# Expert weights in 12 places instead of 19 after the second block, with the side work as a background task

## The chip, the cores and the metric

The kernel runs on one core of a Trainium2 chip. The metric is the device time of one execution in microseconds (us), the median of three runs. Engines: PE is TensorE (matrix products), PEld its weight loads, DVE is VectorE, ACT is ScalarE, POOL is GpSimd, and SP is SyncE, whose queue issues the weight loads. Each engine executes its own instructions in the order in which the program lists them. Everything is float32.

## What is computed

A first block of two layers (a mixer, a cross attention to a memory of 256 rows, and a mixture of 32 experts) and a second block of four layers (pooling, neighbourhood attention, convolution, pooling), on 256 rows of width 1024. What the change touches is below: the cross attention's keys and values of `mem`, the experts, and the pooling layer of the second block's context `ctx`, which depends on no result of the first block.

```python
def memory_cross_attention(x, mem, wq, wk, wv, wo):
    q = to_heads(x @ wq, XATTN_HEADS)
    k = to_heads(mem @ wk, XATTN_HEADS)
    v = to_heads(mem @ wv, XATTN_HEADS)
    logits = jnp.einsum('bhqd,bhmd->bhqm', q, k).astype(jnp.float32) * (XATTN_HEAD_DIM ** -0.5)
    p = jax.nn.softmax(logits, axis=-1).astype(v.dtype)
    return from_heads(jnp.einsum('bhqm,bhmd->bhqd', p, v)) @ wo
...
def hierarchical_moe(x, w_group, b_group, w_expert, b_expert, w_gate, w_up, w_down):
    def one_sequence(xs):
        s = xs.shape[0]
        g_logits = (xs @ w_group + b_group).astype(jnp.float32)
        g_idx = jnp.argmax(g_logits, axis=-1)
        g_weight = jnp.take_along_axis(jax.nn.softmax(g_logits, axis=-1), g_idx[:, None], axis=-1)
        e_logits = (xs @ w_expert + b_expert).astype(jnp.float32).reshape(s, N_GROUPS, EXPERTS_PER_GROUP)
        e_logits = e_logits[jnp.arange(s), g_idx]
        top_val, top_idx = lax.top_k(e_logits, TOP_K_IN_GROUP)
        top_w = jax.nn.softmax(top_val, axis=-1) * g_weight
        expert_id = g_idx[:, None] * EXPERTS_PER_GROUP + top_idx
        gates = jnp.einsum('ske,sk->se', jax.nn.one_hot(expert_id, N_EXPERTS, dtype=jnp.float32), top_w).astype(xs.dtype)
        hid = jax.nn.silu(jnp.einsum('sd,edf->sef', xs, w_gate)) * jnp.einsum('sd,edf->sef', xs, w_up)
        return jnp.einsum('sef,efd->sd', hid * gates[:, :, None], w_down)

    return lax.map(one_sequence, x)
...
def first_block(x, mem, ...):
    ...
    for l in range(DEPTH):
        ...
        x = layer_norm(DEEPNORM_ALPHA * x + mix, ln_mix_g[l], ln_mix_b[l])
        xa = memory_cross_attention(x, mem, xattn_wq[l], xattn_wk[l], xattn_wv[l], xattn_wo[l])
        x = layer_norm(DEEPNORM_ALPHA * x + xa, ln_mem_g[l], ln_mem_b[l])
        ff = hierarchical_moe(x, router_group_w[l], router_group_b[l], router_expert_w[l], router_expert_b[l],
                              expert_w_gate[l], expert_w_up[l], expert_w_down[l])
        x = layer_norm(DEEPNORM_ALPHA * x + ff, ln_ffn_g[l], ln_ffn_b[l])
    return x
...
def _pool_mixer(h, w_in, w_grp, scale, w_out):
    u, g = jnp.split(h @ w_in, 2, axis=-1)
    b_, l_, _ = u.shape
    ug = u.reshape(b_, l_, N_POOL_GROUPS, POOL_GROUP)
    pooled = jnp.stack([_centred_mean(ug[:, :, i], w) for i, w in enumerate(POOL_WINDOWS)], axis=2)
    mixed = jnp.einsum('blgc,gcd->blgd', pooled - ug, w_grp).reshape(b_, l_, WIDTH)
    return (mixed * scale * jax.nn.silu(g)) @ w_out
...
def second_block(x, c, ctx, c_ctx, ...):
    last_ctx_reader = max([i for i in range(DEPTH_2) if i % N_MIXERS_2 == 1], default=-1)
    for i in range(DEPTH_2):
        kind, j = i % N_MIXERS_2, i // N_MIXERS_2
        update_ctx = i < last_ctx_reader
        shift, scale, gate = _modulation(c, ada_w[i], ada_b[i])
        hx = _rmsnorm(x, norm_g[i]) * (1.0 + scale[:, None]) + shift[:, None]
        if kind == 1 or update_ctx:
            cshift, cscale, cgate = _modulation(c_ctx, ada_w[i], ada_b[i])
            hc = _rmsnorm(ctx, norm_g[i]) * (1.0 + cscale) + cshift
        if kind == 0:
            yx = _pool_mixer(hx, pool_w_in[j], pool_w_grp[j], pool_scale[j], pool_w_out[j])
            if update_ctx:
                yc = _pool_mixer(hc, pool_w_in[j], pool_w_grp[j], pool_scale[j], pool_w_out[j])
        elif kind == 1:
        ...
        x = x + gate[:, None] * yx
        if update_ctx:
            ctx = ctx + cgate * yc
    return _rmsnorm(x, final_g)
```

## The kernel before

**Products.** A float32 weight is split into a high and a low part (`whi` by ACT, `wlo` by DVE, L307 and L308), the activations likewise (`xth`, `xtl`), and TensorE makes three products of them. The experts' weights (`w`) are used without a split, in one product. Sums land in PSUM banks; while the experts run, four banks hold the result (`acc`), two serve the main work (`ps`) and two the side work (`pl`).

**Weights.** All weights come in granules of 1 MiB (128x2048), in a fixed order, the plan, which is the order in which the program asks for them. `pump` (line 265) issues a load on the SP queue for each next granule as long as `place` (line 259) finds a place for it. A ring has 8 places, a second ring (`ring2`) 7, and there are 4 boxes. `in_ring2` and `in_box` (lines 249 and 252) give the latter two to expert granules alone, and only if the granule's part of its stage, by `part` (line 255), fits the present one. An expert's gate, up and down are three granules. `used` (line 275) frees a place once the instruction that reads it last has been written, and calls `pump`, so that a load is issued behind those instructions, and waits for them on the chip.

**An expert stage.** `moe(l)` (line 1487) runs once per layer, l = 0 and 1, here the first and the second stage. It has eight blocks (`q`), each with the four experts of one group. For each block TensorE does the gate and up products (128 matmuls, `xg`), the gather of the rows of the next block (`disp`, `xp`), some small transposes, and the down products (`w`, `y`) that add into `acc`. A block takes up to 32 rows an expert at once. If an expert has more, an extra round runs under an `If` (L1537 for gate and up, L1586 for down), whose branches are executed on every engine.

While the first four blocks run, the 8 + 4 + 7 = 19 places are open. At `q == 3` (line 1547) the right side of SBUF is closed and reopened with a pool of split weights (6 pairs) and one of 16 half rows (`more`); in the second stage the boxes are closed and reopened too. From there on there are 12 places. The test in `part` puts the same border into the plan: the gate and up granules of expert 16 and later and the down granules of expert 12 and later belong to a stage's second half.

**Side work.** In the first stage this is `mem_early`: the memory's transposes and its K and V products for the second layer. In the second stage it is `ctx_in` and `pool_ctx`: the whole pooling layer of the context, up to the transposed context (`ctn`) that the neighbourhood layer starts from. `between(n)` (line 1505) runs one piece of it at written places: pieces 9, 11, 13, 15, 17 and 19 in the first stage, 3, 6, 7 and 10 to 21 in the second, where n = 3q stands behind the gate and up of block q, 3q + 1 behind its gather and 3q + 2 behind its down. All of it is written ahead of the last block's down.

**Order elsewhere.** `Flow` (line 86) writes the program as tasks that yield a modelled cost and a lag, and takes the ready task of the lowest priority number. A task that is not ready gives way to another. The modulation products (`ada`, L366 with `w,cT`) are such tasks with priority 2. Two of them concern the change: the last third of `ada(0)` is held until the first router (`ev_router[0]`), and `ada(1)` is spawned at `q == 7` of the first stage.

## Time and profile before

| | |
|---|---|
| median of 3 runs | 1782.72 us (1778.27 to 1784.91) |
| profiled execution | 1784.17 us, its span 1782.4 us |
| PE busy | 1585.1 us, 89% of the span |
| PEld busy | 1230.3 us, 69% |
| DVE busy | 925.4 us, 52% |
| ACT busy | 701.8 us, 39% |
| POOL busy | 166.2 us, 9% |
| DMA | 427.14 MB, mean 240 GB/s |

The span is the time that the profiler saw from the first instruction to the last; the execution's own time has 1.8 us around it. Shares of busy time are means over stages with different limits. The first expert stage lies between 312.69 and 578.17 us, the second between 861.22 and 1198.71 us. In a timeline row the second number is the time from the start of a group of like instructions to its end, and the bracket tells how long the engine was idle ahead of it and what ended that. [...]

### The profile page before, as it was taken

To read this page: it belongs to the slowest core of one execution; us is meant where nothing else is said; L and a number is where in the kernel's file an instruction comes from. 1 tells how busy PE (TensorE), PEld (TensorE's weight loads), DVE (VectorE), ACT (ScalarE), POOL (GpSimd) and SP (SyncE) were. 2 spreads that over 40 slices of the span, in tenths; PEclk is the share of its full clock that TensorE was granted. 3 is DMA by queue.
4 is the path that set the end of the run, shared out by engine and by line. 5 is a ranking of instruction groups with operands and counts; after the bars stand their busy time and mean duration, and the time that the engine had idled before them with its cause. 6 is when DMAs were issued, how large, how long until landed. Compare 5 with 4: busy or idle time off the path is not lost. (4 is left out here: it accounts for less than half of the span.)

```text
span 1782.4 us, 29217 instructions
## 1 busy us (share of the span) xinstructions
PE 1585.1 (89%) x11357; PEld 1230.3 (69%) x11357; DVE 925.4 (52%) x2162; ACT 701.8 (39%) x1422; POOL 166.2 (9%) x248
## 2 busy tenths in 40 slices
PE   7999997778898699989688898978999998999997
PEld 6766986555664566677555576748978886699786
DVE  5567646262132846665321324358455566566645
ACT  4654541112221354433011232344545565445543
POOL 5000301000000400030100000001002122000101
PEclk9989998999999899899799999999999999999999
DMA  8356657899978945476459598796458765575630
GB/s 307 96 189 214 204 221 288 361 395 384 409 284 336 371 150 172 142 269 243 201 205 410 228 410 340 309 407 226 143 165 180 157 114 70 174 275 168 242 100 24
DMA packets 145951, 427.14 MB, mean 240 GB/s; under 512 B 12252, under 2 KB 19652, under 8 KB 121172
## 3 DMA queue, kind: packets, MB, share of 16 engines
q1 hardware_dynamic: 140660, 411.19, 62.1%
q0 software_dynamic: 5088, 13.32, 5.6%
q8 instruction: 118, 1.93, 0.4%
q14 instruction: 85, 0.70, 0.1%
HBM read 423.43 MB, written 1.05 MB: 238 GB/s over the span
## 5 line engine op out<-in xcount | busy, mean ns | idle before, releaser
L308 DVE TENSOR_TENSOR wlo<-w,whi 128x512 fp32r<-128x512 f32 (+2 forms) x586 | 394.7, 709 | 260.0 <-ACT whi L307 257.6
L307 ACT CAST whi<-w 128x512 fp32r<-128x512 f32 (+2 forms) x592 | 341.4, 610 | 241.7 <-PE ps L366 193.1
L366 PE MATMUL ps<-xth,whi 128*128 128x256 f32 x896 | 262.4, 293 | 7.2 <-DVE x L1610 3.8
L366 PE MATMUL ps<-xth,wlo 128*128 128x256 f32 x896 | 257.7, 288 | 4.9 <-DVE wlo L308 4.9
L366 PE MATMUL ps<-xtl,whi 128*128 128x256 f32 x896 | 257.5, 287 | 0.8 <-DVE xtl L1146 0.8
L366 PE MATMUL ps<-whi,xth 128*128 128x512 f32 (+2 forms) x512 | 207.1, 405 | 4.4 <-ACT whi L307 4.0
L366 PE MATMUL ps<-wlo,xth 128*128 128x512 f32 (+2 forms) x512 | 199.2, 389 | 0.4 <-DVE wlo L308 0.4
L366 PE MATMUL ps<-whi,xtl 128*128 128x512 f32 (+2 forms) x512 | 198.9, 388 | 0.2 <-DVE xtl L1146 0.2
L366 PEld LDWEIGHTS ps<-xth,whi 128*128 128x128 f32 x896 | 174.4, 195 | 16.6 <-ACT whi L307 10.6
L366 PEld LDWEIGHTS ps<-xth,wlo 128*128 128x128 f32 x896 | 173.4, 194 | 5.8 <-DVE wlo L308 5.8
L366 PEld LDWEIGHTS ps<-xtl,whi 128*128 128x128 f32 x896 | 173.6, 194 | 3.4 <-issue 1.4
L366 PEld LDWEIGHTS ps<-whi,xth 128*128 128x128 f32 x512 | 99.4, 194 | 32.4 <-ACT whi L307 6.5
L366 PEld LDWEIGHTS ps<-whi,xtl 128*128 128x128 f32 x512 | 98.8, 193 | 20.7 <-DVE xtl L1146 0.9
L366 PEld LDWEIGHTS ps<-wlo,xth 128*128 128x128 f32 x512 | 99.4, 194 | 18.3 <-DVE wlo L308 1.4
L366 PE MATMUL ps<-w,xg 128*32 128x256 f32 x1536 | 90.8, 385 | 10.4 <-issue 3.7
L366 PE MATMUL ps<-w,y 128*32 128x512 f32 (+1 forms) x784 | 80.0, 546 | 8.5 <-DVE y L1455 4.9
L366 PEld LDWEIGHTS ps<-w,xg 128*32 128x32 f32 x1536 | 52.7, 111 | 47.9 <-issue 9.6
L1439 DVE TENSOR_TENSOR y<-y,ps 128x256 f32<-128x256 f32 x12 | 5.1, 422 | 120.8 <-ACTq L1537 76.9
L1146 POOL TENSOR_TENSOR xtl<-aff,xth 128x512 fp32r<-128x512 f32 x9 | 11.6, 1287 | 600.6 <-ACT xth L1145 600.6
L366 PE MATMUL ps<-disp,xp 128*128 128x128 f32 x384 | 52.5, 301 | 16.2 <-DVEq L1537 6.8
L366 PEld LDWEIGHTS ps<-disp,xp 128*128 128x128 f32 x384 | 50.7, 215 | 20.0 <-issue 13.3
L366 PEld LDWEIGHTS ps<-w,y 128*32 128x32 f32 x784 | 25.2, 113 | 50.6 <-issue 36.0
(517 smaller groups left out, 2510.7 us busy)
## 6 DMA issues: line engine op xcount, KB each, us to landing
w<-in_expert_w_gate_dram SPq DMA_DIRECT2D x64, 1024.0 KB, 14.2
w<-in_expert_w_up_dram SPq DMA_DIRECT2D x64, 1024.0 KB, 16.0
w<-in_expert_w_down_dram SPq DMA_DIRECT2D x64, 1024.0 KB, 11.4
w<-in_ada_w_dram SPq DMA_DIRECT2D x48, 1024.0 KB, 5.7
w<-in_pool_w_in_dram SPq DMA_DIRECT2D x24, 1024.0 KB, 11.0
w<-in_na_w_in_dram SPq DMA_DIRECT2D x24, 1024.0 KB, 6.3
w<-in_w_in_dram SPq DMA_DIRECT2D x16, 1024.0 KB, 11.4
w<-in_conv_w_in_dram SPq DMA_DIRECT2D x16, 1024.0 KB, 5.8
```

Source lines behind the costliest of these rows:

```text
L307: self.nc.scalar.copy(hi, src)
L308: (self.nc.gpsimd if self.spare and k % 2 else self.nc.vector).tensor_tensor(lo, src, hi.bitcast(F32), OP.subtract)
L366: self.nc.tensor.matmul(out, lhsT, rhs, start=start, stop=stop, skip_group_check=True)
L1146: (nc.gpsimd if j == 2 else nc.vector).tensor_tensor(lo, fs[j - 1], hi.bitcast(F32), OP.subtract)
L1439: nc.vector.tensor_tensor(h, sg, p[:, 256:512], OP.mult)
```

## The change

`SWITCH = 1`: the pools change behind the second block's gate and up (`q == 1`), no longer behind the fourth's, and `part` moves its border to gate and up of expert 8 and down of expert 4. From there 12 places serve the other six and a half blocks. `landing`, `landed` and `arrival` model when a granule arrives: 2.35 us after the one before it, or 2.2 + 2.35 us after its place came free, whichever is later. Ahead of each block's gate and up the main task yields until eight granules have arrived by that model, and ahead of the down until four have. The side work is no longer written in pieces at given places: `mem_early` and `pool_ctx` (which takes in `ctx_in`) are tasks of priority 2, spawned at the switch, that run where the main task yields. At the end of a stage the main task waits until the side task is written. Splits ahead of their use (`_ahead`) are allowed by the modelled landing. The last third of `ada(0)` has no hold, and `ada(1)` is spawned at the start of the second layer. Outside the expert stages one set of eight PSUM banks takes the place of two sets of four.

```diff
@@ -31,12 +31,13 @@
+SWITCH = 1
+DMA_STEP = 2.35
+DMA_LAG = 2.2
...
-EARLY_V = True
-MEM_AT = (9, 11, 13, 15, 17, 19)
@@ -254,7 +256,7 @@
-        return 2 * key[2] + (key[3] >= (12 if key[1] == "expert_w_down" else 16))
+        return 2 * key[2] + (key[3] >= 4 * SWITCH + (0 if key[1] == "expert_w_down" else 4))
@@ -262,6 +264,34 @@
+    def got(self):
+        return len(self.rec) if self.plan is None else self.n_get
+    def landing(self):
+        self.base = self.got()
+        self.freed, self.lands = [], [self.flow.now] * 4
+    def landed(self, n):
+        n -= self.base
+        t = self.lands[-1]
+        for k in range(len(self.lands), n + 1):
+            j = k - RING - PERM
+            known = j < len(self.freed)
+            t = max(t, (0.0 if j < 0 else self.freed[j] if known else self.flow.now) + DMA_LAG) + DMA_STEP
+            if known:
+                self.lands.append(t)
+        return self.lands[n] if n < len(self.lands) else t
+    def arrival(self, n):
+        while True:
+            t = self.landed(self.got() + n - 1)
+            if t <= self.flow.now + 0.2:
+                return
+            yield 0, t - self.flow.now
@@ -274,6 +304,10 @@
+        self.freed.append(self.flow.now)
+        self.free(i)
+    def free(self, i):
@@ -311,12 +345,12 @@
-            self.used(i)
+            self.free(i)
...
-            if self.keep and self.unit_list[self.n_unit][0] > self.n_get + 1:
+            if self.keep and self.landed(self.unit_list[self.n_unit][0]) > self.flow.now:
@@ -337,6 +371,8 @@
+        if k == 3:
+            self.freed.append(self.flow.now)
@@ -345,16 +381,6 @@
-    def piece(self, gen):
-        while True:
-            self.flow.lane = "pl"
-            v = next(gen, None)
-            self.flow.lane = "ps"
-            if v is None:
-                return
-            yield v
@@ -1179,28 +1205,25 @@
-        mem = self.mem_rows()
-        yield
+        mem = self.mem_rows(self.T)
...
+        yield 0, 8.0
...
-        yield 1.8, 0
-        yield
+        del mem
+        yield 1.8, 0.8
...
-            yield
-        if EARLY_V:
...
-                yield
@@ -1500,23 +1523,14 @@
-        side = [self.ctx_in(), self.pool_ctx()] if l else [self.mem_early()]
-        def between(n):
-            if l == 0:
-                if n in MEM_AT:
-                    self._ahead()
-                    yield from self.piece(side[0])
-            elif n in (3, 6, 7):
-                yield from self.piece(side[0])
-            elif 10 <= n <= 21:
-                self._ahead()
-                yield from self.piece(side[1])
+        side = prep = None
...
+            if side:
+                yield from self.arrival(8)
+                self._ahead()
@@ -1544,7 +1558,7 @@
-            if q == 3:
+            if q == SWITCH:
@@ -1556,19 +1570,26 @@
-            yield 8.5, 0
-            yield from between(3 * q)
+                self.landing()
+                side = self.flow.spawn(self.pool_ctx() if l else self.mem_early(), 2)
+                side.lane = "pl"
+                if not l:
+                    self.t_mem = side
+            yield 7.5, 0
+            if side:
+                self._ahead()
...
-                yield 5.0, 0 if q > 2 else 3.0
-                yield from between(3 * q + 1)
+                yield 4.8, 0.5
...
-            if q == 7 and not l:
-                self.adas.append(self.flow.spawn(self.ada(1), 2, 6.0))
+                yield 0.4, 0.5
+            if side:
+                yield from self.arrival(4)
+                self._ahead()
@@ -1599,8 +1620,6 @@
             if q == 7:
-                self._ahead()
-            if q == 7:
                 st = [self.s("bn", [P, 2, 6], bufs=2) for _ in range(2)]
@@ -1609,14 +1628,14 @@
-            yield 6.0, 0 if q > 2 else 10.0
-            yield from between(3 * q + 2)
-            if q == 2 and l == 0:
-                yield prep.done
+            yield 6.0, 0 if side else 8.0
+        if prep:
+            yield prep.done
+        yield side.done
...
-        self.psums(ps=4, ps2=4)
+        self.psums(ps=8)
@@ -2096,7 +2115,7 @@
-                self.adas.append(flow.spawn(self.ada(0, (Event(), self.ev_router[0])), 2, 8.0))
+                self.adas.append(flow.spawn(self.ada(0), 2, 8.0))
@@ -2123,19 +2142,20 @@
+            self.adas.append(flow.spawn(self.ada(1), 2, 6.0))
...
-            if l == 0:
...
-        mem = flow.spawn(mem_kv(), 0)
+        mem = self.t_mem if l else flow.spawn(mem_kv(), 0)
@@ -2161,36 +2181,33 @@
-    def load_ctx(self):
...
-    def ctx_in(self):
-        ctx = self.load_ctx()
-        yield
...
+    def pool_ctx(self):
...
+        ctx = self.load_ctx(self.T)
+        yield 0, 8.0
...
-        yield
-        self.ctx_n = self.normed(ctx, ss, True)
...
-    def pool_ctx(self):
...
-        ct = yield from self.mod_t(self.ctx_n, mc, 1, self.more, 0, [self.T("aff") for _ in range(4)])
+        yield 0, 4.0
+        ctx = self.normed(ctx, ss, True)
+        ct = yield from self.mod_t(ctx, mc, 1, self.more, 2.0, [self.T("aff") for _ in range(4)])
+        del ctx
...
-        yield
@@ -2229,14 +2242,12 @@
-            yield
...
-                if b and nh:
-                    ctx_n = self.normed(rows, ss, True)
-                if b or nh:
-                    yield
-        self.ctn = yield from self.mod_t(ctx_n, self.mods[1], 1, self.more, 0, [self.T("aff") for _ in range(4)])
+        del ct, yt
+        yield 0, 3.0
+        ctx = self.normed(rows, ss, True)
+        self.ctn = yield from self.mod_t(ctx, self.mods[1], 1, self.more, 2.0, [self.T("aff") for _ in range(4)])
```

The order of the instructions shows it in three places. On the SP queue in the second expert stage, before: the end of the first block's down (L1590 to L1586), the loads issued there, and the `If` of the second block's gate and up (L1537).

```order
L1590 UNCONDITIONAL_BRANCH
L1589 UNCONDITIONAL_BRANCH
L1586 UNCONDITIONAL_BRANCH
L246 DMA w_10904<-in_expert_w_gate_dram 128x2048
L246 DMA w_10906<-in_expert_w_up_dram 128x2048
L246 DMA w_10908<-in_expert_w_up_dram 128x2048
L246 DMA w_10910<-in_expert_w_up_dram 128x2048
L1537 COMPARE_AND_BRANCH
```

The same place after, where L1607 is the end of the first block's down and L1551 the `If` of the second block's gate and up:

```order
L1607 UNCONDITIONAL_BRANCH
L1551 COMPARE_AND_BRANCH
L1554 COMPARE_AND_BRANCH
L1555 COMPARE_AND_BRANCH
L1555 UNCONDITIONAL_BRANCH x2
L2359 BRANCH_PREFETCH_HINT
L1555 REGISTER_ALU
L1555 COMPARE_AND_BRANCH
L1555 UNCONDITIONAL_BRANCH
L1554 UNCONDITIONAL_BRANCH
L1551 UNCONDITIONAL_BRANCH
L248 DMA w<-in_expert_w_gate_dram 128x2048 x4
```

Four loads stood between the first down and the second gate and up; now none does, and the loads of the third block follow behind the second block's `If`.

On TensorE at the end of the second expert stage, before: the end of the last block's down (L1586), and behind it products of the neighbourhood layer's context (`xth`, `xtl` of `ctn`).

```order
L1590 UNCONDITIONAL_BRANCH
L1589 UNCONDITIONAL_BRANCH
L1586 UNCONDITIONAL_BRANCH
L366 MATMUL ps<-xth,whi 128x256
L366 MATMUL ps<-xtl,whi 128x256
L366 MATMUL ps<-xth,wlo 128x256
```

After: the first of these rows are the last of 24 products of `pool_w_out` (`yt`), which begin directly behind the end of the last down; then the transposes of the context, and the same products as before.

```order
L392 MATMUL pl<-whi,yt 128x512 x2
L392 MATMUL pl<-wlo,yt 128x512
L392 MATMUL pl<-whi,yt 128x512
L395 MATMUL pl<-ident,ctx 128x128 x16
L392 MATMUL ps<-xth,whi 128x256
L392 MATMUL ps<-xtl,whi 128x256
```

The last part of the context's pooling layer moved behind the last down, and stands ahead of the 168 products of the neighbourhood layer's context.

On DVE at the same place, before: the splits of the next weights, then the residual and the statistics of `x`.

```order
L1586 UNCONDITIONAL_BRANCH
L308 TENSOR_TENSOR wlo<-w,whi 128x512 x4
L1610 SCALAR_TENSOR_TENSOR x<-xp_10128,acc 128x512
L1071 BN_STATS bn<-x 128x6
L1610 SCALAR_TENSOR_TENSOR x<-xp_10129,acc 128x512
L1071 BN_STATS bn<-x 128x6
```

After: the end of the norm of `x` (L1094), then the splits, then the gate and the sum of the context (`gy`, `ctx`), and its norm.

```order
L416 SCALAR_TENSOR_TENSOR rs_z<-rs_t,rs_z 128x2
L1094 TENSOR_SCALAR x<-x,mv,rs_z 128x1024 x2
L342 TENSOR_TENSOR wlo<-w,whi 128x512 x8
L1770 TENSOR_TENSOR gy<-pl,gate 128x512
L1771 TENSOR_TENSOR ctx<-ctx,gy 128x512
L1770 TENSOR_TENSOR gy<-pl,gate 128x512
L1771 TENSOR_TENSOR ctx<-ctx,gy 128x512
L1745 TENSOR_TENSOR rms_v<-rms_ss 128x2
```

The splits moved from ahead of the residual of `x` to behind its norm, and the context's last steps stand behind them.

## Rows read from the trace of the kernel before

**Rows 1.** Windows by stage: us, busy PE, PEld, DVE, ACT, POOL, PEclk, DMA share, GB/s.
```profile
312.69:578.17 265.48, 220.19 (x2145) 148.57 (x2144) 81.14 (x220) 51.48 (x95) 2.97 (x8) 0.95 0.90 362
861.22:1198.71 337.49, 295.53 (x2788) 205.20 (x2788) 108.32 (x260) 87.00 (x165) 8.87 (x14) 0.97 0.78 308
1198.71:1231.51 32.80, 24.95 (x168) 24.38 (x169) 30.08 (x65) 13.10 (x28) 6.67 (x4) 0.84 0.81 280
```

**Rows 2.** Windows of 25 us, columns as in rows 1.
```profile
200.00:225.00 25.00, 25.00 (x147) 21.96 (x146) 12.47 (x19) 12.45 (x23) 0.00 (x0) 1.00 0.66 211
325.00:350.00 25.00, 18.47 (x204) 11.53 (x202) 6.72 (x21) 2.50 (x5) 0.00 (x0) 0.96 1.01 419
875.00:900.00 25.00, 20.40 (x276) 15.45 (x280) 3.64 (x11) 3.17 (x5) 0.00 (x0) 0.93 0.01 1
```

**Rows 3.** Timeline of PE: start us, duration us, engine, line, out<-in, count, [idle <-releaser].
```profile
933.19 7.11 PE L366 MATMUL pl<-w,xg 128*32 128x256 f32 x128 [1.11 <-issue]
941.45 3.81 PE L366 MATMUL ps<-disp,xp 128*128 128x128 f32 x32 [1.15 <-DVEq L1537]
...
947.12 1.92 PE L366 MATMUL ps<-w,y 128*32 128x512 f32 x16 [0.56 <-issue]
...
954.13 7.11 PE L366 MATMUL ps<-w,xg 128*32 128x256 f32 x128 [0.78 <-DMA w<-in_expert_w_down_dram]
```

**Rows 4.** Timeline of PE behind each layer's cross attention and first expert stage.
```profile
283.36 3.64 PE L366 MATMUL ps<-w,cT 128*32 128x512 f32 x32
289.18 0.30 PE L369 MATMUL ps<-ident,x 128*128 128x128 f32 x1 [2.18 <-DVE x L1068]
...
578.32 1.92 PE L366 MATMUL pl<-w,cT 128*32 128x512 f32 x16
...
590.25 0.45 PE L369 MATMUL ps<-ident,x 128*128 128x128 f32 x1 [7.54 <-DVE x L1068]
```

**Rows 5.** DMA issues from 321.3 to 321.6: size, us from issue to landing.
```profile
w<-in_expert_w_up_dram SPq DMA_DIRECT2D x1, 1024.0 KB, 5.5
```

**Rows 6.** Timeline of PE, first expert stage.
```profile
334.99 7.84 PE L366 MATMUL ps<-w,xg 128*32 128x256 f32 x128 [0.49 <-PEq L1586]
...
366.21 1.90 PE L366 MATMUL acc<-y,ct 128*128 128x512 f32 x7 [2.57 <-DVE y L1469]
...
394.93 7.11 PE L366 MATMUL ps<-w,xg 128*32 128x256 f32 x128 [0.49 <-PEq L1586]
...
426.93 1.51 PE L366 MATMUL ps<-w,xg 128*32 128x256 f32 x12 [1.91 <-DMA w<-in_expert_w_up_dram]
```

**Rows 7.** Windows of side work in the second stage, columns as in rows 1.
```profile
1025.47:1036.64 11.17, 11.16 (x52) 8.98 (x56) 4.09 (x8) 2.83 (x5) 0.00 (x0) 1.00 1.02 411
1052.72:1064.47 11.75, 11.75 (x102) 11.62 (x105) 3.13 (x7) 2.79 (x5) 0.00 (x0) 1.00 1.01 418
```

**Rows 8.** Timeline of the SP queue, second stage: start, time to the last issue.
```profile
906.99 25.74 SPq L246 DMA_DIRECT2D w<-in_expert_w_gate_dram  x4
```

**Rows 9.** Timeline of PE, a gather of the fifth block of the second stage.
```profile
1009.30 5.45 PE L366 MATMUL ps<-disp,xp 128*128 128x128 f32 x32 [3.67 <-PEq L1537]
```

**Rows 10.** Timeline of PE behind the last down of the second stage.
```profile
1202.52 0.55 PE L366 MATMUL ps<-xth,whi 128*128 128x256 f32 x1 [3.81 <-DVE x L1610]
...
1231.51 0.33 PE L369 MATMUL ps<-ident,xn 128*128 128x128 f32 x1 [0.36 <-ACT xn L1736]
```

**Rows 11.** Timeline of DVE around the end of the second stage.
```profile
1174.51 0.69 DVE L1751 TENSOR_TENSOR gy<-pl,gate 128x512 f32<-128x512 f32 x1 [3.76 <-PE pl L366]
...
1186.33 0.69 DVE L1146 TENSOR_TENSOR xtl<-aff,xth 128x512 fp32r<-128x512 f32 x1 [0.27 <-ACT xth L1145]
...
1201.36 1.02 DVE L1610 SCALAR_TENSOR_TENSOR x<-xp,acc 128x512 f32<-128x512 f32 x1
...
1210.89 1.53 DVE L1068 TENSOR_SCALAR x<-x,mv,rs_z 128x1024 f32<-128x1024 f32 x2
```

51 lines of the change are left out of this document (25 added, 26 removed).

## The prediction

> **What bounds the kernel now.** I read the windows by stage first. The two expert stages take 265.5 and 337.5 us of the 1782.4 us span, and TensorE is busy for 220.2 and 295.5 us of them [rows 1]. So in both the matmuls themselves are the larger part, and a perfect order could win back 45 and 42 us at most. Then the 25 us windows: DMA is at a share of 1.01 (419 GB/s) early in the first stage and at 0.01 early in the second, where every place was full and no expert block had yet been consumed [rows 2]. A 1 MiB granule at 419 GB/s takes 1.0486 / 0.419 = 2.50 us. Then the timeline of one block (four experts) without an extra round: gate/up 7.1 us, 1.15 of waiting, gather 3.8, small transposes, down from 947.12, next gate/up at 954.13: 20.9 us a block, against 12 x 2.5 = 30 us to load one [rows 3]. In the first stage, then, weights and TensorE are close rivals. In the second, which has extra rounds and more side work, TensorE leads.
>
> The change moves no arithmetic in or out; it moves when things happen. I follow it in program order and give times on the scale of the trace of before.
>
> **Part 1, the modulation tasks: +4.** The last third of ada(0) loses its hold. Before, its 16 matmuls (32 passes, 3.64 us) and an 8-pass gsel group ran after the cross attention, where TensorE would anyhow have waited for the layer norm: it still idles 2.18 us behind them [rows 4]. Now they stand inside the attention, where a 25 us window shows TensorE busy for 25.00 [rows 2]. Likewise the first four granules of ada(1) ran from 578.32, with 7.54 us of idling behind them [rows 4]; now they run in mixer 1. Lower bound 0 (all of it finds holes), upper bound 3.64, 1.9 for the gsel group (by the row of 1.92) and 4.4 (578.32 to 590.25 less the 7.54) = 9.9; I take 4, nearest the first of these three, since that window is full. The eight-bank PSUM pool rotates as the two alternating pools of four did: 0, either way.
>
> **Part 2, first expert stage: +3.** After an idle queue a granule lands 5.5 us after its issue [rows 5], each further one 2.5 later. Up to the second block's gate/up (end 334.99 + 7.84 = 342.8 [rows 6]) loads are as before. Then only one place is free, where before seven more were: its granule lands by 357, and DMA idles until the second down frees four at 366.21 + 1.90 = 368.1 [rows 6], where before it ran at 1.01 [rows 2]. That costs 11 us of loading. Third block: its down lands by 381, in time. After its gate/up, three wk granules are queued ahead of the fourth block's weights, which land by 408. TensorE meanwhile has sixteen memory transposes (3 us, at under the 0.30 of a single one [rows 4]) and 144 K matmuls. Some 96 fill 11.75 us [rows 7], so 144 take 17.6, with the splits 18.6: it reaches the fourth gate/up at 417, 22 us later than before (394.93 [rows 6]), with 22 us of side work done. No loss. The fifth starts at 459, 40 us later than before, again with the side work of that time done. Sixth: TensorE is ready at 486, the last up lands at 491: 5 lost. Seventh: no side work is left; ready at 511, landed at 521: 9.5 lost. This block has an extra round, so its eight places come free only at 541, and the queue, full since 531, idles 11 us; the eighth starts at 564, 3 after TensorE was ready. It ends at 581.6, against 578.17 [rows 1]: +3.4. What the kernel before lost to weights was little (1.91 us in the fifth block [rows 6]). Bounds: DMA never idle from 321.4, 85 granules x 2.5 + 5.5 and a last down of 6.2 (947.12 to 954.13 less 0.78 [rows 3]) end at 546, less than reachable, so below I go to -8; granules at 2.6 us (403 GB/s, a little under the 411 of the slower window of rows 7), +10.
>
> **Part 3, second expert stage up to its last down: +4.** Here the new part() rule bites. The third block's weights may not use the four boxes or ring2 of the old stage, and the ring is full with the second down. So the SP queue has no load between the first and the second gate/up [the order above], and all eight wait for 940.3, the end of the second gate/up (933.19 + 7.11 [rows 3]). Before, they were issued from 906.99 on [rows 8] and the third gate/up began at 954.13. Now: issue about 941.9, first landing 947.4, eighth 964.9: 10.8 us with nothing queued on TensorE, since the context transposes stand behind the third down. Then, as in part 2: about 3 us between context transposes and their first product (vector work once hidden behind a down), 6 us before the sixth gate/up, 1 before the eighth. Against that, 24 matmuls of pool_w_out (5.6 us, half of the 48 that fill 11.16 us [rows 7]) and 16 transposes (3) leave the stage for its tail, and about 7 of the 42 us of idling are filled. Sum 10.8 + 3 + 6 + 1 - 8.6 - 7 = +5; the block by block account gives +4, which I take: last down's products end at 1202.8, not 1198.7. Bounds: -6 (15 filled, and no wait before the sixth), +12 (nothing filled).
>
> At waits of this size the trace shows the matmul clock falling: the gather after 3.67 us of idling took 5.45 us [rows 9] instead of 3.81 [rows 3], 1.6 more. [...] The change adds some six such waits and ends about three: +2, bounds 0 and 8. [...]
>
> [...]
>
> **Part 4, behind the second stage: +19.** This is the dear one. Before, the pool's context branch was finished ahead of the last down; 3.8 us after it TensorE started 168 matmuls of the neighbourhood layer's context, and transposed xn at 1231.51, 32.8 us after [rows 10]. Now the last pool_w_out granule, the second context norm and its transposes come after it, and TensorE's order puts all 168 behind them. On DVE the residual and norm of x go first: from 1201.36 to 1212.4 they took 11.1 us [rows 11]. Only then come the splits of that granule. With e the end of the last products: splits from e + 11.4, the 24 matmuls until e + 18 (5.6 us), gate and add, rms chain, transposes, affine and the first low half until e + 29 (the same steps from 1174.51 to 1187.0 took 12.5 with a gate/up between, I take 11 [rows 11]), the 168 until e + 52 (20.6 by the 11.75 for 96 [rows 7]; 29 with the splits competing, 1202.52 to 1231.51 [rows 10]; I take 23, since here more splits are done ahead). So xn's transposes come at e + 52 instead of e + 32.8: +19. Bounds +15 and +27. It stays lost: 222 groups of TensorE work follow in an unchanged order, and xn itself is ready by about then.
>
> **Sum.** 4 + 3 + 4 + 2 + 19 = +32. The profiled execution took 1784.17 us, 1.45 above the median of the runs, 1782.72; 1784.2 + 32 = 1816.2 is 1814.7 on the median's scale: 1815.
>
> **Rivals.** (a) Faster: the background work does fill the waits, and 12 places are enough. What speaks for it: one block's 30 us of loading exceeds its 20.9 of matmuls, and every product that fills the difference is free. If DMA ran on from 321.4 without the stalls of 11, 7 and 11 us, the first stage would end near 550, four over that bound (-28); with the tail and part 1 as above and part 3 at 0 the sum is -28 + 4 + 19 = -5, and if the x chain also gives way to the context in the tail, -20: 1763. It needs TensorE to reach each gate/up before the four down granules are loaded; the seventh block with its extra round does not.
> (b) About the same, 1785: the tail's order costs only the TensorE work moved there (8.6), because the 168 matmuls overlap the x chain after all, and the first stage gains 5. Against it: TensorE executes in order, and the first product needs a split behind eleven microseconds of DVE work.
> (c) Much slower, 1840: with fewer places the one block per stage with an extra round stalls the queue, and the stall passes on to each later block: part 2 at +10, part 3 at +12, tail +27, clock +6, part 1 +4 are +59 at the extreme, 1842. It decides once granules take 2.6 us and TensorE reaches the later gate/ups always after the queue has drained.
> (d) The change does nothing, because the order hardly moves: excluded, since the order shows it moved.
>
> **Chances.** Forecast 0.62 (own range 1800 to 1830), (a) 0.12, (b) 0.13, (c) 0.13. A measurement of this kernel tells about 0.5% (8.9 us) from no change. Faster by more than that is (a) but for its worse end: 0.10. Within 0.5%: the rest of (a) and most of (b): 0.12. Slower: 0.78. The range for 8 in 10 is the forecast's own, widened to half of (b) and most of (c): 1786 to 1837.
>
> **What would show it.** In the changed profile: DMA near 0 for some 10 us before the third down of the first stage and a 10 us idle before the third gate/up of the second, ended by DMA; TensorE idle for 10 to 13 us directly behind the last down of the second stage, ended by DVE or ACT, with 24 pool_w_out matmuls between it and a second idle of some 8 us; xn transposed about 20 us later relative to that down. It is wrong if the second stage's last down comes more than 10 us earlier than now, or if the 168 matmuls start within 10 us of it.

## The result and the profile after

The changed kernel takes 1822.63 us (median of 4 runs, 1819.37 to 1835.5) against 1780.49 for the kernel before on the same chip (4 runs, 1773.2 to 1784.91): the ratio is 1.0251, with a 95% interval from 1.0213 to 1.029. It is slower, by 38 to 52 us. The forecast was 1815, 32 us more than before. The profiled execution took 1822.22 us (span 1819.9), and its span is 37.5 us longer than the span before. The profiled execution of before took 1784.17 us, 4 to 8 us more than the medians of before here and in the experiments, so differences of spans come out smaller than differences of medians.

The 37.5 us, cut at landmarks that both timelines have:

| stretch | before | after | difference | forecast |
|---|---|---|---|---|
| to the first gate/up of the first stage | 312.69 | 319.42 | +6.7 | part 1, with the next-but-one row: +4 |
| first stage, to its last products | 265.48 | 267.08 | +1.6 | +3 |
| to the first gate/up of the second stage | 289.53 | 288.38 | -1.1 | (part 1) |
| second stage, to its last products | 331.01 | 340.44 | +9.4 | +4, and +2 for the clock |
| to the transposes of xn | 32.80 | 53.99 | +21.2 | +19 |
| to the end | 550.9 | 550.6 | -0.3 | 0 |

The windows of the changed kernel, with the columns of [rows 1] (in brackets behind a busy time its count of instructions; PEclk is the granted clock of TensorE as a share of its full speed):

```profile
319.42:586.50 267.08, 222.27 (x2145) 148.04 (x2144) 82.20 (x220) 52.68 (x97) 2.95 (x8) 0.94 0.88 352
874.88:1215.32 340.44, 292.42 (x2717) 197.64 (x2716) 95.67 (x227) 77.21 (x146) 5.53 (x9) 0.95 0.73 289
1215.32:1269.31 53.99, 33.20 (x210) 29.63 (x209) 41.75 (x98) 22.19 (x46) 9.26 (x9) 0.81 0.64 223
```

The second window of before from its own first gate/up (in [rows 1] it begins with the gather):

```profile
867.70:1198.71 331.01, 289.05 (x2757) 198.81 (x2756) 108.32 (x260) 86.42 (x164) 8.87 (x14) 0.97 0.77 306
```

In the second stage TensorE idles 48.0 us after (340.44 less 292.42) and 42.0 before. It is busy for 3.4 us longer with 40 matmuls fewer, at a granted clock of 0.95 instead of 0.97.

The wait ahead of the third block, forecast from the order of SP's queue, is there. SP's timeline of the changed kernel, which answers to [rows 8], and TensorE's at the third gate/up, which answers to the last row of [rows 3]:

```profile
913.47 2.09 SPq L248 DMA_DIRECT2D w<-in_expert_w_down_dram  x4
949.08 2.22 SPq L248 DMA_DIRECT2D w<-in_expert_w_gate_dram  x4
951.34 1.92 SPq L248 DMA_DIRECT2D w<-in_expert_w_up_dram  x4
```

```profile
962.91 0.82 PE L392 MATMUL ps<-w,xg 128*32 128x256 f32 x6 [0.92 <-PEq L1607]
965.60 5.60 PE L392 MATMUL ps<-w,xg 128*32 128x256 f32 x62 [1.87 <-DMA w<-in_expert_w_gate_dram]
973.07 0.62 PE L392 MATMUL ps<-w,xg 128*32 128x256 f32 x2 [1.87 <-DMA w<-in_expert_w_up_dram]
975.57 5.33 PE L392 MATMUL ps<-w,xg 128*32 128x256 f32 x58 [1.88 <-DMA w<-in_expert_w_up_dram]
```

Nothing is issued from 915.56 to 949.08. The gate/up takes 18.0 us to 980.90 where 7.11 are its work: 10.9 are lost, 5.6 of them in three waits for DMA and the rest in matmuls that run slower between the waits. The granted clock is 1.00 in the 6 matmuls ahead of the first of these waits, 0.70 in the 62 behind it and 0.68 in the last 58, over the whole stretch 0.81:

```profile
962.91:980.90 17.99, 12.36 (x128) 5.85 (x128) 0.00 (x0) 0.00 (x0) 0.00 (x0) 0.81 1.01 419
```

TensorE behind the last down, which answers to [rows 10]:

```profile
1227.12 0.80 PE L392 MATMUL pl<-wlo,yt 128*128 128x512 f32 x1 [11.03 <-DVE wlo L342]
...
1241.43 2.37 PE L395 MATMUL pl<-ident,ctx 128*128 128x128 f32 x8 [6.30 <-ACT ctx L1755]
...
1245.71 0.53 PE L392 MATMUL ps<-xth,whi 128*128 128x256 f32 x1
...
1269.31 0.33 PE L395 MATMUL ps<-ident,xn 128*128 128x128 f32 x1 [0.36 <-ACT xn L1755]
```

Two waits, 11.03 and 6.30 us, stand ahead of the 168 products, which begin 30.4 us behind the last down instead of 3.8. Ahead of the first stage TensorE waits longer for the norm than in [rows 4]:

```profile
295.28 0.45 PE L395 MATMUL ps<-ident,x 128*128 128x128 f32 x1 [5.75 <-DVE x L1094]
```

In the first stage the sixth and seventh gate/up wait for weights, as forecast; and two windows show DMA at rest, ahead of the second down's end and during the seventh block's extra round:

```profile
492.47 4.94 PE L392 MATMUL ps<-w,xg 128*32 128x256 f32 x58 [1.86 <-DMA w<-in_expert_w_up_dram]
...
521.34 0.62 PE L392 MATMUL ps<-w,xg 128*32 128x256 f32 x2 [1.86 <-DMA w<-in_expert_w_up_dram]
```

```profile
365.00:371.00 6.00, 5.41 (x40) 2.17 (x31) 4.78 (x13) 1.38 (x2) 0.00 (x0) 1.00 0.10 40
531.00:542.00 11.00, 10.18 (x152) 7.57 (x156) 1.50 (x6) 0.58 (x1) 0.00 (x0) 1.00 0.05 18
```

### The profile page after: what moved, and what is told of

The parts are those of the page before. It is cut to its first block, busy times and chain, and to the rows that moved or that the text cites. A ratio compares the mean times of both kernels' runs of the same rounds, so it can differ in the third digit from the quotient of the medians.

```text
span 1819.9 us, 29205 instructions
## 1 busy us (share of the span) xinstructions
PE 1602.6 (88%) x11357; PEld 1235.4 (68%) x11357; DVE 924.0 (51%) x2162; ACT 702.4 (39%) x1422; POOL 161.5 (9%) x248
## 5 line engine op out<-in xcount | busy, mean ns | idle before, releaser
L392 PE MATMUL ps<-w,xg 128*32 128x256 f32 x1792 | 113.2, 400 | 19.8 <-DMA w<-in_expert_w_up_dram 14.7
L392 PEld LDWEIGHTS ps<-w,xg 128*32 128x32 f32 x1792 | 63.1, 115 | 67.8 <-DMA w<-in_expert_w_up_dram 19.0
L392 PE MATMUL ps<-w,y 128*32 128x512 f32 (+1 forms) x960 | 91.1, 514 | 5.2 <-issue 2.8
L392 PE MATMUL ps<-disp,xp 128*128 128x128 f32 x416 | 56.2, 298 | 28.2 <-DVEq L1551 6.7
L1461 ACT ACTIVATE y<-ps 128x256 f32<-128x256 f32 x17 | 6.5, 383 | 186.3 <-PE ps L392 178.0
```

The costliest lines, as they stand in the source:

```text
L392: self.nc.tensor.matmul(out, lhsT, rhs, start=start, stop=stop, skip_group_check=True)
L1461: nc.scalar.activation(sg, p[:, 0:256], AF.Silu)
```

## The experiments

Each was timed beside the kernel before, whose median was 1776 to 1779 us in these runs; times of stretches are from the profiled executions. The intervals of the ratios are wide: those of all variants of the changed kernel with 12 places, but for the one with three cures, overlap the interval of the changed kernel itself. What a variant shows therefore rests on its stretch of the profile first, and on the medians second. "The leftover" is what the changed kernel has behind the last down of the second stage: 24 products of `pool_w_out`, the second norm of the context and its 16 transposes.

**The places alone.**

```diff
-            if q == 3:
+            if q == 1:
...
-        return 2 * key[2] + (key[3] >= (12 if key[1] == "expert_w_down" else 16))
+        return 2 * key[2] + (key[3] >= (4 if key[1] == "expert_w_down" else 8))
```

> The kernel before with the change of the pools alone moved to the second block, and the border of the parts with it; the side work stays in its written pieces, all ahead of the last down. Theory (fewer places cost time by themselves, and background work only hides it): the first stage loses 5 to 15 us, since blocks three and four wait for weights with no side work written there, the second stage 10 to 16, the stretch behind the last down stays at 33 us, and the whole is 15 to 28 us slower than before, about 1802 us. Rival (the places cost nothing, all of the loss is the leftover side work and ada): within 6 us of before, 1780 us.

Measured: 1802.81 us, ratio 1.014 (1.0079 to 1.02), about 25 us slower. Its windows of the two stages:

```profile
313.50:584.37 270.87, 221.70 (x2145) 146.99 (x2144) 81.33 (x220) 51.48 (x95) 2.96 (x8) 0.97 0.87 351
873.50:1211.15 337.65, 290.57 (x2757) 197.53 (x2756) 108.18 (x260) 86.31 (x164) 8.88 (x14) 0.97 0.76 301
```

The first stage lost 5.4 us, the second 6.6 (10 to 16 were expected), and the stretch behind it stayed at 32.79. The fourth gate/up of the first stage took 17.9 us and the third of the second 16.3, instead of 7.11, with waits for weights in both:

```profile
397.86 0.71 PE L366 MATMUL ps<-w,xg 128*32 128x256 f32 x2 [1.76 <-DMA w<-in_expert_w_up_dram]
...
967.36 0.62 PE L366 MATMUL ps<-w,xg 128*32 128x256 f32 x2 [1.88 <-DMA w<-in_expert_w_up_dram]
```

Fewer places cost time by themselves; the rival that they are free falls. The spans differ by 15.8 us, 10 less than the medians: its own profiled execution is the shortest of its four, and that of before lies above its median.

**A place for the third block's weights.**

```diff
         room = ["box"] if self.in_box(key) else ["ring2"] if self.in_ring2(key) else []
+        if key[:3] == ("E", "expert_w_down", 1) and key[3] < 4:
+            room = []
```

> The changed kernel, in which the first block's four down granules of the second stage may use only the ring, so that four ring places come free with the first down and the third block's four gate granules are loaded ahead of the second gate/up. Theory (the third block waits because its weights had no place until the second gate/up was done): the third gate/up of the second stage, which took 18.0 us from 962.91 to 980.90, takes 7 to 9 us, and the whole is 8 to 11 us faster than the changed kernel, about 1812 us. Rival (a later wait takes the time back, since 12 places bound the stage as a whole): the third gate/up is short, but the last down of the stage comes less than 4 us earlier, 1819 us or more.

Measured: 1811.85 us, ratio 1.0187 (1.0126 to 1.0247), 11 us faster than the changed kernel. SP issues the four gate granules early, and TensorE's timeline shows a third gate/up of 8.5 us:

```profile
937.08 2.01 SPq L248 DMA_DIRECT2D w<-in_expert_w_gate_dram  x4
```

```profile
958.78 4.09 PE L394 MATMUL ps<-w,xg 128*32 128x256 f32 x70 [0.75 <-PEq L1609]
963.63 3.64 PE L394 MATMUL ps<-w,xg 128*32 128x256 f32 x58 [0.76 <-DMA w<-in_expert_w_up_dram]
```

The stage took 330.81 us instead of 340.44, and from the end of the third gate/up to the last products 234.5 instead of 234.4: the 9.6 us stayed won, and the rival (a later wait takes them back) falls.

**The hold on ada(0).**

```diff
-                self.adas.append(flow.spawn(self.ada(0), 2, 8.0))
+                self.adas.append(flow.spawn(self.ada(0, (Event(), self.ev_router[0])), 2, 8.0))
```

> The changed kernel with the hold on the last third of ada(0) back, as in the kernel before. Theory (its 32 passes and the gsel group stand on the path inside the cross attention and filled a wait behind it before): the first gate/up of the first stage begins at 312.7 instead of 319.4 us, 6 us earlier, and the whole is 5 to 7 us faster, about 1816 us. Rival (the attention absorbs them and the 6.7 us come from the PSUM pool of eight banks or from elsewhere): the first gate/up stays at 318 us or later and the whole within 2 us.

Measured: 1814.76 us, ratio 1.0205 (1.0139 to 1.027), 8 us faster than the changed kernel. The first gate/up began at 313.15. With the hold it begins at 310.2 to 314.2 in all profiled kernels (eight, mean 312.6), without at 315.1 to 320.4 (six, mean 317.3). Four of the eight have the set of eight PSUM banks, as the six without the hold do; they begin at 310.2 to 313.7 (mean 312.0), so the rival that the PSUM pool costs the time falls. The hold is worth some 5 us (4.7 against all eight, 5.4 against these four), and the 6.7 of the table hold some spread of single executions.

**The leftover added to the kernel before.**

```diff
-            elif 10 <= n <= 21:
+            elif 10 <= n <= 19:
                 self._ahead()
                 yield from self.piece(side[1])
+            elif n == 23:
+                for _ in range(2):
+                    self._ahead()
+                    yield from self.piece(side[1])
```

> The kernel before, in which the last two pieces of the context's pooling layer (the last 24 products of pool_w_out with the second norm, and its transposes) are written behind the last down instead of ahead of it, which is the end that the changed kernel has. Theory (what is left over behind the last down is dear because its chain runs through DVE and TensorE executes in order): from the end of the last products to the transposes of xn it takes 50 to 55 us instead of 32.8, the stage ahead of it becomes 6 to 9 us shorter, and the whole is 10 to 15 us slower, about 1790 us. Rival (the chain costs the same wherever it stands, as the kernel that wrote all of it ahead of the last block suggests): what the stage gains equals what the end loses, within 4 us of before.

Measured: 1791.59 us, ratio 1.0055 (1.0023 to 1.0086), 4 to 15 us slower. TensorE, behind last products that end at 1193.54:

```profile
1193.80 0.50 PE L366 MATMUL pl<-whi,yt 128*128 128x512 f32 x1 [0.26 <-ACT whi L307]
```

```profile
1244.58 0.33 PE L369 MATMUL ps<-ident,xn 128*128 128x128 f32 x1 [0.36 <-ACT xn L1740]
```

The stretch took 51.0 us instead of 32.8, the stage 3.4 less (6 to 9 were expected): the leftover alone costs some 15 us between these landmarks, as the medians have it (14.7). Here the products of `pool_w_out` begin at once, since their splits were done ahead, but TensorE then waits in front of the context's transposes:

```profile
1216.54 2.37 PE L369 MATMUL pl<-ident,ctx 128*128 128x128 f32 x8 [16.48 <-ACT ctx L1740]
```

On DVE the residual and the norm of x stand ahead of the context here too (1196.20 to 1207.28), now between its splits and its sum. The changed kernel has 11.03 and 6.30 us of waiting, this one 16.48 in one piece: splits that are done ahead moved the wait and did not remove it.

**DVE's order at the end turned round.** The leftover stays behind the last down, but is written ahead of the residual of x.

```diff
             for _, i in wd:
                 self.used(i)
+            if q == 7 and l:
+                yield side.done
             if q == 7:
```

> The changed kernel, in which the rest of the context's pooling layer is still written behind the last down of the second stage, but ahead of the residual and the norm of x, so that DVE's queue has the context's splits first. Theory (TensorE's idle 11.03 us behind the last down is the residual and norm of x standing ahead of the splits in DVE's queue): the 24 products of pool_w_out begin within 4 us of the last down instead of 11.3, the transposes of xn come 6 to 10 us earlier, and the whole is 6 to 10 us faster than the changed kernel, about 1814 us. Rival (x's own chain, some 30 us from its residual to xn in the kernel before, then starts 18 to 20 us later and becomes the bound): the products begin early but xn comes no earlier than 51 us behind the last down, and the whole stays within 3 us of the changed kernel.

Measured: 1817.87 us, ratio 1.0215 (1.0155 to 1.0275). TensorE behind last products that end at 1208.17:

```profile
1208.44 0.50 PE L392 MATMUL pl<-whi,yt 128*128 128x512 f32 x1 [0.27 <-ACT whi L341]
...
1221.07 2.37 PE L395 MATMUL pl<-ident,ctx 128*128 128x128 f32 x8 [6.36 <-ACT ctx L1757]
...
1230.91 0.55 PE L392 MATMUL ps<-xth,whi 128*128 128x256 f32 x1 [4.21 <-DVE x L1631]
```

```profile
1260.19 0.33 PE L395 MATMUL ps<-ident,xn 128*128 128x128 f32 x1 [0.56 <-ACT xn L1757]
```

The 11.03 are gone, and the 168 products begin 22.7 us behind the last down instead of 30.4, but xn comes at 52.0 instead of 54.0: the rival holds. The 168 products now wait for the residual of x, which reads the PSUM banks of `acc` that they are to use; in the kernel before the same reader ends the 3.81 us of [rows 10]. They also take 28.7 us instead of 23.2; for 3.62 us of that they wait for splits, which stand behind the norm of x on DVE. DVE has the context's chain and that of x one after the other, whichever is first, and is busy for most of the stretch:

```profile
1208.17:1260.19 52.02, 35.41 (x209) 32.12 (x209) 42.49 (x96) 21.96 (x46) 12.95 (x11) 0.77 0.66 227
```

DVE's 42.49 us here are 41.75 in the changed kernel; before, they were 30.08 of 32.80 [rows 1]. Of the 5 us in the medians the start makes some 4 (315.1 instead of 319.4).

**The leftover ahead of the last block.**

```diff
+            if q == 7 and l:
+                yield side.done
             if side:
                 yield from self.arrival(8)
```

> The changed kernel, in which the main task of the second expert stage waits until the context's pooling task is written before it writes the last block's gate and up; the 24 products of pool_w_out, the second context norm and its 16 transposes then stand ahead of that block. Theory (the time behind the last down is long because the context's chain is left over): the last products to the transposes of xn fall from 54 us to 32 to 36 us; the last gate/up begins about 12 us later; the whole is 8 to 13 us faster than the changed kernel, about 1811 us. Rival (x's own chain on DVE sets the time behind the last down): that stretch stays at 48 us or more and the whole is the same or up to 10 us slower, 1820 to 1832.

Measured: 1827.53 us, ratio 1.0268 (1.0207 to 1.0329): no faster than the changed kernel. Behind the last down it took 30.6 us (32 to 36 were expected), but the last block began 58.3 us behind the seventh instead of 37.7, and TensorE waited in it too:

```profile
1218.96 2.37 PE L395 MATMUL pl<-ident,ctx 128*128 128x128 f32 x8 [6.36 <-ACT ctx L1757]
...
1241.08 5.07 PE L392 MATMUL ps<-w,y 128*32 128x512 f32 x32 [8.76 <-DVE y L1478]
```

The whole is where the rival had it, but not by the rival's mechanism, for the stretch behind the last down is short. The theory that only the place behind the last down is dear falls: in one lump the chain costs as much ahead of the block.

**The context's end spread over the last block.** `pool_w_out` ahead of the last gate/up, the norm and the transposes ahead of its down.

```diff
+            if q == 7 and l:
+                yield self.ev_pool
             if side:
                 yield from self.arrival(8)
...
+            if q == 7 and l:
+                yield side.done
             if side:
                 yield from self.arrival(4)
...
         del ct, yt
+        self.flow.set(self.ev_pool)
         yield 0, 3.0
```

> The changed kernel with the context's end spread over the last block as in the kernel before: pool_w_out ahead of the last gate/up of the second stage, the norm's transposes between it and the last down. Theory (the chain costs only where nothing lies beside it; written in one lump it was exposed ahead of the last block, spread over the block its DVE part lies beside 128 matmuls): behind the last down 31 to 34 us, the last gate/up 9 to 13 us later than in the changed kernel, the whole 5 to 10 us faster than it, about 1815 us. Rival (the chain's cost cannot be hidden in that block, as when all of it stood ahead of the last block): no faster than the changed kernel, 1820 us or more.

Measured: 1823.53 us, ratio 1.0263 (1.0222 to 1.0304): nothing gained; the last block took 31.2 us (before: 23.6). TensorE, and DVE in front of it:

```profile
1227.96 2.37 PE L395 MATMUL pl<-ident,ctx 128*128 128x128 f32 x8 [10.94 <-ACT ctx L1760]
```

```profile
1221.75 2.50 DVE L342 TENSOR_TENSOR wlo<-w,whi 128x512 fp32r<-128x512 f32 x4 [5.41 <-ACT whi L341]
1224.16 0.42 DVE L1478 COPY y<-ps 128x256 f32<-128x256 f32 x1
1224.50 0.15 DVE L1750 TENSOR_TENSOR rms_v<-rms_ss 128x2 f32<-128x2 f32 x1
```

DVE, whose sums were ready at 1210.5, stood idle in front of splits, and the norm stood behind them. So the next run had the norm ahead of the splits:

```diff
-        self.flow.set(self.ev_pool)
-        yield 0, 3.0
         ctx = self.normed(rows, ss, True)
+        self.flow.set(self.ev_pool)
```

> As the run that spread the context's end over the last block, with one difference: the second context norm is written directly behind the sums that feed it, ahead of the splits of the next weights, as the kernel before has it. Theory (in that run the norm stood in DVE's queue behind splits that waited for weights to arrive, and TensorE stood 10.94 us in front of the context's transposes for it): that idle time falls to under 2 us, the last block from 31.2 to 22 to 26 us, and the whole is 6 to 9 us faster than that run and 5 to 9 us faster than the changed kernel, about 1815 us. Rival (the norm's own chain of short DVE steps is what takes the time): the idle time stays at 8 us or more.

Measured: 1816.66 us, ratio 1.0215 (1.0175 to 1.0255), 7 us faster than the run before it and 6 faster than the changed kernel; the last block took 27.0 us, a little more than the 22 to 26 of the theory. The first eight transposes no longer wait, the others do (6.95 us, where the theory had under 2 and the rival 8 or more):

```profile
1216.00 1.04 PE L395 MATMUL pl<-ident,ctx 128*128 128x128 f32 x8
1223.98 1.12 PE L395 MATMUL pl<-ident,ctx 128*128 128x128 f32 x4 [6.95 <-ACT aff L1151]
```

**Three cures at once:** the first of the two spreads, the hold, and the place for the third block.

> The changed kernel with three things at once: the context's end spread over the last block, the hold on ada(0), and the first down of the second stage in the ring. Theory (three separate losses that add): 6 + 7 + 10 us faster than the changed kernel, about 1798 us, that is still 15 to 22 us slower than before. Rival (with fewer places the stage is bound as a whole, so a wait removed comes back at the next block): 1806 us or more.

Measured: 1807.25 us, ratio 1.0165 (1.012 to 1.0211), 15 us faster than the changed kernel: by the number the rival holds (1806 or more), though only just. The single runs gave 11, 8 and -1 us, 18 in sum: what was measured is near that sum and short of the 23 that I had put down, above all because the spread alone gave nothing. That waits removed came back elsewhere is not shown.

**19 places, and the background task.** `SWITCH = 3`, with the hold and the spread.

> The changed kernel with the pools changed behind the fourth block (19 places until then, as before), the hold on ada(0), and the context's end spread over the last block; what is left of the change is the background task in place of written pieces. Theory (the places cost time, the background task itself is no worse than pieces in the first stage, but in the second it starts as late as the pools change and fills only modelled waits, so that its work piles up ahead of the last block): the first stage takes 258 to 268 us, the second 5 to 15 us more than before, the whole about 1788 us. Rival A (the background task is the better filler): 1772 us or less. Rival B (the places don't matter): 1800 us or more, as with 12 places.

Measured: 1802.97 us, ratio 1.0146 (1.0107 to 1.0185). The windows of the two stages:

```profile
310.20:566.10 255.90, 216.05 (x2145) 146.81 (x2144) 82.38 (x220) 52.76 (x97) 3.03 (x8) 0.95 0.92 371
855.30:1215.96 360.66, 299.85 (x2757) 205.05 (x2756) 110.98 (x264) 89.22 (x168) 8.92 (x14) 0.94 0.73 286
```

The whole misses the theory (1788) by 15 us and lies where rival B had it, but the first stage denies its reason, that the places don't matter. The first stage is 9.6 us shorter than before, a little below the forecast: there the background task is the better filler, if it has the places. The second is 30 us longer (27 counted to xn) instead of 5 to 15: the context's work piled up ahead of the last block, which began 80 us behind the seventh (35 before). Four kernels side by side, in us:

| | pieces, 19 places (before) | pieces, 12 places | task, 12 places (changed) | task, 19 places |
|---|---|---|---|---|
| first stage | 265.5 | 270.9 | 267.1 | 255.9 |
| first gate/up of the second stage to xn | 363.8 | 370.4 | 394.4 | 391.0 |

In the second row the places are worth 7 us at most and the task, with its modelled arrivals, costs 24 to 27. The last kernel has its context's end spread as well, so its 391.0 hold that too.

**The first stage of that with the second stage of before**, first with the other small edits of the change, then with nothing else (both keep written pieces in the second stage):

```diff
-SWITCH = 1
+SWITCH = 3
...
-                side = self.flow.spawn(self.pool_ctx() if l else self.mem_early(), 2)
+                if not l:
+                    side = self.flow.spawn(self.mem_early(), 2)
...
+            yield from between(3 * q)
...
```

> A mixture: the first expert stage with the background task and modelled arrivals, but with 19 places until the fourth block (it took 255.9 us so), the hold on ada(0) as before, and the second stage with its written pieces as in the kernel before. Theory (in the first stage the background task gains about 10 us when the places are kept, and in the second the pieces end its context in time): first stage 254 to 260 us, second stage 328 to 334, 31 to 34 behind it, the whole 6 to 12 us faster than before, about 1768 us. Rival (the first stage's gain is given back in the mixer of the second layer, whose loads then start earlier but wait for the same engines): within 3 us of before.

> The kernel before with one thing of the change: in the first expert stage the side work is a background task that fills the waits for modelled arrivals, with 19 places until the fourth block; all else, the second stage and its order of instructions included, as before. Theory (the mixture before this one had its first stage right, 256 us, and lost in the second to waits behind Ifs that its other order brought): first stage 254 to 258 us instead of 265.5, second stage 328 to 334 us, the whole 6 to 10 us faster than before, about 1771 us. Rival (the waits behind Ifs in the second stage come with any shift of the code or of the loads, and take the gain): second stage 338 us or more, the whole within 3 us of before or slower.

Measured: 1784.97 us, ratio 1.0028 (1.001 to 1.0046), and 1782.17 us, ratio 1.002 (0.9997 to 1.0043). Neither beats the kernel before. The first stages took 256.3 and 257.6 us, as expected, the second 343.3 and 334.1; the first mixture lost its gain there and not between the stages (286.7 us instead of 289.5), so its rival's reason falls. The second kernel's row of the second block, where [rows 3] has 1.15 us of waiting and 3.81 of gather:

```profile
938.35 5.44 PE L402 MATMUL ps<-disp,xp 128*128 128x128 f32 x32 [5.12 <-PEq L1571]
```

It has 7.9 us less in the first stage and 3.0 more in the second, and its span is 3.7 us shorter; the ratio shows none of it. Against a before whose runs spread from 1768 to 1791, whether a gain of some 4 us is left is not settled.

## Why the prediction came out as it did

**Bound and parts.** The forecast of +32 was right in direction and near in size: +37.5 of span, +42 of the medians. The likeliest case came true, none of the rivals. Against the parts, the span came out 1.6 us higher in part 1, 1.4 lower in part 2, 3.4 higher in part 3 and 2.2 higher in part 4.

**Part 1: +4, measured +5.6 in the table.** The hold is worth some 5 us by the means over fourteen kernels, and the wait behind the attention that its work had filled grew from 2.18 to 5.75 us, in line with the working. The stretch between the stages, into which ada(1) moved, came out 1.1 shorter.

**Part 2: +3, measured +1.6.** The blocks came 3 to 8 us earlier than worked out from the fourth on, and the waits at the sixth and seventh were where forecast. Of the two rests of the load queue, the one of the seventh block was the 11 us of the working, the one ahead of the second down's end 6 us (a share of 0.10 from 365 to 371) instead of 11. The working had places and task in one number; the runs take them apart: 12 places alone cost 5.4, the task gives 3.8 of it back, and with the old places it gains 9.6.

**Part 3: +4 and +2 for the clock, measured +9.4.** The 10.8 us at the third gate/up were 10.9, and a place for four granules took 9.6 us off the stage. That they agree so closely is in part luck: the sign that the prediction named, 10 us of idling ahead of that gate/up, did not come. It began after 0.92 us and took 18.0, with 5.6 us of waiting in it and 5.3 of slower matmuls: its 128 matmuls were busy 12.36 instead of 7.11 us while their granules came one by one. Behind it the two stages, the kernel before first:

```profile
961.24:1198.71 237.47, 208.33 (x1792) 146.93 (x1790) 88.34 (x196) 73.13 (x137) 6.71 (x10) 0.97 0.87 344
980.90:1215.32 234.42, 204.90 (x1751) 143.13 (x1750) 75.69 (x163) 63.92 (x119) 3.37 (x5) 0.96 0.86 343
```

All but the third gate/up came to -1.5 us, 1.6 ahead of it and -3.1 behind it, where the terms of the sum give 3 - 8.6 + 2 = -3.6. Idling outside it rose by 0.4 us instead of 3 (3, 6 and 1 of new waits less 7 filled). What was mis-sized is the term for the clock, +2 with bounds 0 and 8, read from two gathers of the kernel before (granted clock 0.69 in the one of 5.45 us, 1.00 in the one of 3.81): 40 matmuls left, an estimated 8.6 us by the working, and yet TensorE is busy only 1.9 us less outside the third gate/up, so matmuls ran some 6.7 us slower there, 1.5 ahead of it and 5.2 behind it. Which waits that belongs to, and whether all of it is the clock, is not shown.

**Part 4: +19, measured +21.2: the right number by half a mechanism.** I let the products wait for splits behind DVE's norm of x. They did, 11.03 us, the second wait of some 8 us was 6.30, and the 168 products began 30.4 us behind the end of the last products, where I had 29. But I took the order on DVE for the cost, and it is not: with the splits done ahead (the run that added the leftover to the kernel before) or DVE's order turned round, the stretch still took 51.0 and 52.0 us. What these three kernels share is that two chains run one after the other through DVE, ACT and TensorE: the context's (24 products to the first product of `ctn`) and that of x (residual to xn). The leftover adds some 12 us of DVE work (41.6 to 42.5 us busy in the three, 30.08 before) to a stretch in which DVE was busy for nine tenths, and 7 to 10 us more in which DVE waits. Before, the context's chain was finished under the last block. And the gain is not had by moving the lump: the two runs that wrote it ahead of or in the last block gave back there what they won behind it, and the run with the norm ahead of the splits kept some 6 of 24 us.

**Rivals.** (a) named the right ingredient: the first stage can come down to 256 us, but with 19 places, not with 12. (b) had the tail cost only the 8.6 us of TensorE work moved there; it cost 21.2. (c) expected stalls that pass on to later blocks; the third block's did not, for with its cure the blocks behind it took as long (234.5 and 234.4 us).

## What to carry to other kernels

Fewer weight places can cost time where the set of places changes, because loads meant for the new set must wait for the old one to empty (10.9 us here): look for a stretch of the load queue without issues, and give the next block's first granules a place that survives the change. Side work that fills waits must be finished under other work before the stage ends: a serial chain over several engines cost most of its length in one lump here, both ahead of the last block (which began 20.6 us later) and behind it (a stretch 21.2 us longer). When a wait is removed at such an end, look for the place it moves to (here the same engine's queue, 16.48 us, or the PSUM banks that the next products need, 4.21 us) before counting it as a gain.

## What the hardware showed that was not expected

Waits of TensorE's sequencer behind an `If` (PEq) last up to 5.12 us and move between kernels. At the second block of the second stage [rows 3] has 1.15 us, put down to DVE's sequencer; four other kernels have 4.28 to 5.12 there, put down to TensorE's own, with a gather of 5.4 to 6.5 us behind it instead of 3.81. In the 6 us around the wait of 5.12 the DMA view lists a packet of instructions among the weight loads:

```profile
q8 instruction: 1, 0.02, 1.1%
```

Such a packet stands at that place in the changed kernel too, whose wait there is 1.15 us, so the trace does not decide whether the two belong together. What sets the length of these waits stays open. In the two mixtures the wait and the gather at this place take 6.6 and 5.6 us more than before, about the lower end of the gain that was looked for.
